# Second layer of a hybrid transformer: the compressed keys and values are worked out earlier, the router's weights and the compressed scores later

## Chip, cores and metric

The kernel runs on one core of a Trainium2 chip. The metric is the device time of one execution in microseconds (us). The kernel before took 1400.51 us as the median of three runs (1397.81 to 1400.72).

## What is computed

Two transformer layers over 256 tokens of width 1024, all in fp32. The first layer has two kinds of attention and a dense feed-forward part. The second layer, which the change touches, has block attention (heads `cq`, `ck`, `cv`), sparse attention in three branches (queries `dq`; compressed, selected and windowed keys), and a mixture of eight experts, two per token. Cut to the second layer:

```python
cq, ck, cv, dq, dkc, dvc, dks, dvs, dkw, dvw, dg = split_cols(x @ w_in, ODD_SIZES)
o_c = moba_attention(rope(cq), rope(ck), cv)
k_cmp = compress_blocks(dkc[:, tok_idx], pe[0], phi_w1[0], phi_w2[0])   # 15 blocks of 32 tokens
v_cmp = compress_blocks(dvc[:, tok_idx], pe[1], phi_w1[1], phi_w2[1])   # gelu(rows @ w1) @ w2
p_c   = masked_softmax(q @ k_cmp * scale)                               # compressed scores
o_d   = g0 * (p_c @ v_cmp) + g1 * selected(dq, dks, dvs) + g2 * window(dq, dkw, dvw)
x     = layer_norm(ALPHA * x + concat(o_c, o_d) @ w_out)
x     = layer_norm(ALPHA * x + moe(x))     # router logits, top 2 of 8 experts, swiglu of width 3584
```

With 256 tokens the selected and the windowed branch each see all causal keys.

## The kernel before

Every large matrix product is made from split operands: each weight tile of 128x1024 fp32 is loaded into a raw buffer (`raw`, `load_raw`, L123), cast to fp32r on ScalarE (`wh`, L150), and the rest is subtracted on VectorE (`wl`, L152). TensorE then makes three products per weight chunk (`mm3`, L160: L164, L165, L166) into one PSUM bank per 128 tokens. There are two groups of 128 tokens, t = 0 and t = 1. `project` (L293) does this for one slice of the input weights `od_w_in` and hands each bank to a `consume` function (`c_kv`, `c_dq`, `c_w`, `c_rope`), which applies the rotary embedding on VectorE and GpSimd, turns the result with TensorE transposes (`hps`) and copies it out.

In the second layer the calls stand at L907 to L929: the projection of keys and values (`c_kv`, 4 raw tiles), of the sparse queries (`c_dq`, 4), `router_weights` (L847: the layer norm's gain and shift rows are turned on TensorE, `rtps`, and multiplied with the router's matrix, `rsps`, both only needed for the router much later), the projection of the window's keys and values with the gates (`c_w`, 3 raw tiles: 420, 420 and 280 KB), `compress` (L704), `compressed` (L782: scores `cps` against the compressed keys, softmax into `ec`), the projection of `ck`, the start of the sparse attention (`nsa_start`, L808: scores `sps`, exp on ScalarE, turned probabilities `ptps`, product `oT`), the projections of `cq` and `cv`, the output weights, and so on to the router and the experts.

`compress` has three steps. The rows are formed: 32 small products with a selection matrix (`kp`, L710), a ScalarE copy (`km`, L714), eight VectorE copies into the gathered rows (`xr`, L721), two GpSimd operations for the border columns. Then 64 records of products with the hidden weights `phi_w1` (`hp`, L731), whose 8 raw tiles of 512 KB are loaded here (L729). Then a copy (`cmp_hs`, L734), a fold (`ht`, L737), the gelu on VectorE and ScalarE, and the products `kc` and `vc` (L757, L764), which the end of the sparse attention (`nsa_end`, L815) needs.

Three resources set the order. Raw tiles come from two pools of 4 and 6 buffers and go round (first four indices of every ten to the pool of 4): a load waits until a buffer of its pool is free, that is until the tile that was in it has been subtracted (or, for `phi_w1`, multiplied). All raw loads are issued on SyncE's one queue, in order; a load that waits holds up those behind it. The order of instructions on each engine is not the program text's: a planner puts them in order ahead of time from its own estimate of when each is ready, with earlier program text preferred. On the chip each engine then runs its list in that order. PSUM tiles outside the projections share two buffers of tag `at` (`kp`, `hp`, `ht`, `kc`, `vc`, `rsps`, `rtps`, `cps`, `ptps`) and two of tag `sp` (`hps`, `sps`).

After the second layer's attention the experts run: 672 raw tiles of 512 KB, which stream in as long as raw buffers come free.

Of the kernel before, what the change touches and what calls it, by code (L numbers as in the profile page):

```python
# [39 lines left out]
def hybrid_kernel(ctx, tc, x, ev_w_in, ev_w_out, dif_lambda, dif_subln, ffd_w_gate, ffd_w_up, ffd_w_down,  # L40
# [82 lines left out]
    def load_raw(src, kt, n):  # L123

        raws = []
        step = max(1, min(kt, 1024 // n))
        for k0 in range(0, kt, step):
            kk = min(step, kt - k0)
            raw = raw_tile()
            rv = raw[:, :kk * n]  # L130
            ld = nc.sync.dma_start(rv.rearrange("p (k n) -> p k n", n=n),
                                   src[k0 * P:(k0 + kk) * P, :].rearrange("(k p) n -> p k n", p=P))
            loads.append(ld.ins)
            raws.append((rv, kk, n))
        return raws
# [4 lines left out]
    def split_w(raws, after=()):  # L140


        ps_ = []
        for i, (rv, kk, n) in enumerate(raws):
            w = kk * n
            pool = split_pools[nsplit[0] % len(split_pools)]
            nsplit[0] += 1
            wh = pool.tile([P, 1024], F32R, tag="wh", name="wh")
            wl = pool.tile([P, 1024], F32R, tag="wl", name="wl")
            nc.scalar.copy(wh[:, :w], rv)  # L150
            with behind(after[i] if i < len(after) else None):
                nc.vector.tensor_tensor(wl[:, :w], rv, wh[:, :w].bitcast(F32), ALU.subtract)  # L152
            for k in range(0, w, n):
                ps_.append((wh[:, k:k + n], wl[:, k:k + n]))
        return ps_
# [101 lines left out]
    def bank(shape=(P, 512), name="bk"):  # L257
        return at.tile(list(shape), F32, tag="sp" if name in TAGS else "at", name=name)

    def mbank(name, tag="mm"):  # L260
        return mm.tile([P, 512], F32, tag=tag, name=name)
# [31 lines left out]
    def project(xp, src, n, consume, raws=None, after=()):  # L293
        w = split_w(raws or load_raw(src, KD, n), after)
        for t in range(NT):
            ps = mbank("mmps")
            mm3(ps[:, :n], list(zip(xp[t], w)))
            consume(t, ps)
# [52 lines left out]
    def pairs_of(r):  # L351
        return [r[:, i * P:(i + 1) * P] for i in range(r.shape[-1] // P)]
# [67 lines left out]
    xp = [x_parts(xt[:, t]) for t in range(NT)]  # L420
# [32 lines left out]
    def c_rope(to, dst, scaled, gqa=False):  # L453
        def f(t, ps):
            r = roped()
            rope(ap, ps, 8, t, r, scaled, gqa)
            to(dst, pairs_of(r), t)
        return f
# [120 lines left out]
    with more_split("splitf", "right", NSPLIT), mkpool("ffn") as fp, more_raw("rawf", NEXTRA):  # L579
# [25 lines left out]
        for k0, t in steps:  # L605
# [6 lines left out]
            if k0 + 2 == KF:  # L612
# [5 lines left out]
                if t == 0:  # L618
                    xp = [x_parts(x2[:, 0])]
# [13 lines left out]
    w1 = od_w_in[0]  # L633
# [9 lines left out]
    ckB = blocks_tile(lp, 4, "ckB")  # L643
# [57 lines left out]
            nc.vector.tensor_tensor(fold[r], ident[r, q * 32:q * 32 + 30],  # L701
                                    ident[r, q * 32 + 30:q * 32 + 31].to_broadcast([32, 30]), ALU.add)

    def compress():  # L704
        kp = bank((P, 2, 2, P), "kp")
        for z in range(2):
            for g in range(2):
                for t in range(NT):
                    for a in range(2):
                        nc.tensor.matmul(kp[a * 64:a * 64 + 64, z, g, t * 64:t * 64 + 64],  # L710
                                         kvc[:, t, z * P + g * 64:z * P + g * 64 + 64], selm[:, a],
                                         start=True, stop=True)
        km = ap.tile([P, 2, 2, P], F32, tag="rope_u", name="km", bufs=2)
        nc.scalar.copy(km, kp)  # L714
        xr = lp.tile([P, 2, 16, 32], F32, tag="e", name="xr", bufs=NE_)
        nc.gpsimd.memset(xr[:, :, :, 31], 0.0)
        nc.gpsimd.tensor_copy(xr[:, :, :, 30], peT.rearrange("p (z k) -> p z k", z=2))
        for z in range(2):
            for g in range(2):
                for jj in range(2):  # L720
                    nc.vector.tensor_copy(  # L721
                        xr[:, z, 8 * jj:8 * jj + 8, g * NCMP:(g + 1) * NCMP],
                        km[:, z, g].rearrange("p (n j) -> p j n", j=8)[:, :, jj:jj + NCMP])
        hp = bank((P, 2, S), "hp")
        for z in range(2):
            for q in range(4):
                raw = raw_tile()
                rv = raw.rearrange("p (k n) -> p k n", n=S)
                nc.sync.dma_start(rv, nsa_phi_w1[0, z, q * 512:(q + 1) * 512, :].rearrange("(k p) n -> p k n", p=P))  # L729
                for k in range(4):  # L730
                    nc.tensor.matmul(hp[k * 32:k * 32 + 32, z], xr[:, z, q * 4 + k], rv[:, k],  # L731
                                     start=q == 0, stop=q == 3, skip_group_check=True)
        hs = ap.tile([P, 2, S], F32, tag="rope_u", name="cmp_hs", bufs=2)
        nc.vector.tensor_copy(hs, hp)  # L734
        ht = bank((P, 4, 32), "ht")
        for m in range(4):
            nc.tensor.matmul(ht[:, m, :30], hs[:, m // 2, m % 2 * P:(m % 2 + 1) * P], fold, start=True, stop=True)  # L737
        hb_ = ap.tile([P, 4, 30], F32, tag="cmp_h", name="cmp_h", bufs=1)
        nc.vector.tensor_copy(hb_, ht[:, :, :30])
        u = ap.tile([P, 4, 30], F32, tag="cmp_u", name="cmp_u", bufs=1)  # L740
        nc.vector.tensor_tensor(u, hb_, hb_, ALU.mult)
        nc.vector.tensor_scalar(u, u, 0.044715, 1.0, op0=ALU.mult, op1=ALU.add)
        nc.vector.tensor_tensor(u, u, hb_, ALU.mult)
        nc.vector.tensor_scalar(u, u, -40.0, None, op0=ALU.max)
        nc.scalar.activation(u, u, AF.Exp, scale=-2.0 * math.sqrt(2.0 / math.pi))
        nc.vector.tensor_scalar(u, u, 1.0, None, op0=ALU.add)
        nc.vector.reciprocal(u, u)
        nc.vector.tensor_tensor(u, u, hb_, ALU.mult)
        gr = lp.tile([P, 2, 2, 4, 32], F32, tag="e", name="gr", bufs=NE_)
        nc.gpsimd.memset(gr, 0.0)  # L750
        nc.gpsimd.tensor_copy(gr[:, :, :, :, :NCMP],
                              u[:, 2:4].rearrange("p m (g n) -> p m g n", g=2)[:, :, :, None, :]
                              .to_broadcast([P, 2, 2, 4, NCMP]))
        kc = bank((P, 32), "kc")
        for g in range(2):
            for m in range(2):
                nc.tensor.matmul(kc[g * 64:g * 64 + 64, :NCMP], w2[:, 0, m], u[:, m, g * NCMP:(g + 1) * NCMP],  # L757
                                 start=m == 0, stop=m == 1)
        for g in range(2):
            nc.vector.tensor_copy(kcB[g * 64:g * 64 + 64, g, :NCMP], kc[g * 64:g * 64 + 64, :NCMP])  # L760
        vc = bank((P, 2, 64), "vc")
        for g in range(2):
            for m in range(2):
                nc.tensor.matmul(vc[:, g], gr[:, m, g].rearrange("p r n -> p (r n)"), w2[:, 1, m],  # L764
                                 start=m == 0, stop=m == 1)
        for g in range(2):
            nc.vector.tensor_tensor(vblk[:, g], vc[:, g, None, :].to_broadcast([P, 4, 64]),
                                    bmask[:, :, None].to_broadcast([P, 4, 64]), ALU.mult)
# [78 lines left out]
    def router_weights():  # L847

        ps = bank((P, 2, NE), "rsps")
        for i, row in enumerate(gb):  # L850
            for k0 in range(0, KD, 4):
                pt = bank((P, 4, P), "rtps")
                for k in range(4):
                    nc.tensor.transpose(pt[:, k], row[:, (k0 + k) * P:(k0 + k + 1) * P], ident)
                rT = lp.tile([P, 4, P], F32, tag="pT", name="rowT", bufs=3)
                evac(rT, pt)
                for k in range(4):
                    nc.tensor.matmul(ps[:, i], rT[:, k], wr[:, k0 + k], start=k0 + k == 0, stop=k0 + k == KD - 1)
                if i == 0:
                    nc.vector.tensor_tensor(gwr[:, k0:k0 + 4], wr[:, k0:k0 + 4], rT[:, :, :NE], ALU.mult)  # L860
        nc.vector.tensor_copy(s1, ps[:, 0])
        nc.vector.tensor_tensor(s0, ps[:, 1], br, ALU.add)
# [42 lines left out]

    rbank = bank
    project(xp, w1[:, 2048:2560], 512, c_kv, None, (normed[-2],) * 3 + (normed[-1],))  # L907
    project(xp, w1[:, 1536:2048], 512, c_dq)
    router_weights()
    project(xp, w1[:, 2560:2840], 280, c_w)  # L910
    compress()
    ec = compressed()
    project(xp, w1[:, 512:1024], 512, c_rope(to_blocks, ckB, False))
    os_ = [nsa_start(qt) for qt in range(NT)]
    project(xp, w1[:, 0:512], 512, c_rope(to_heads, cqT, True))
    project(xp, w1[:, 1024:1536], 512, lambda t, ps: nc.scalar.copy(cv[:, t], ps))
# [391 lines left out]
```

## Time and profile before

| what | value |
|---|---|
| median of three runs | 1400.51 us |
| profiled execution, device time | 1402.62 us |
| its span on the core | 1400.8 us |
| TensorE busy | 1314.0 us (94%) |
| VectorE busy | 754.3 us (54%) |
| ScalarE busy | 544.7 us (39%) |
| bytes moved | 429.98 MB |
| second layer, first projection to first expert's products | about 332 to 519 us of the span |

The profile's times are us from the span's start. Matmuls overlap, so that a row's duration is longer than its distance to the next start; idle time of an engine ahead of an instruction stands in square brackets behind it, with what ended it.

### The profile page before, as it was taken

The page shows a single profiled execution, that of the slowest core. Times are in us where ns is not written, and L with a number is a line of the kernel's source. Part 1 is how long each engine was busy: PE and PEld are TensorE (multiplying, and loading weights), DVE is VectorE, ACT ScalarE, POOL GpSimd, SP SyncE. Part 2 cuts the span into 40 slices and gives each one's busy share as a digit, 9 for nine tenths or more (in the row PEclk, how much of TensorE's full clock was granted, in tenths as well). Part 3 has the DMA queues.
Part 4 walks back from the last instruction along what each step waited for, and adds up shares of the span by engine and source line. Part 5 has one row for each costly group of instructions (what it writes and reads, how often), then busy time and mean ns, then how long its engine had stood idle before and what let it go on. Part 6 is the DMA issues. An engine that isn't in the chain of part 4 may idle for free. (4 is left out here: it accounts for less than half of the span.)

```text
span 1400.8 us, 18207 instructions
## 1 busy us (share of the span) xinstructions
PE 1314.0 (94%) x6136; PEld 848.2 (61%) x6136; DVE 754.3 (54%) x1194; ACT 544.7 (39%) x796; POOL 45.2 (3%) x79
## 2 busy tenths in 40 slices
PE   8979999998988989999999999999998999999983
PEld 7856888886864763367874356884446886432221
DVE  5977655547578561278863057893137895201004
ACT  4454444433436311166652056772034774100000
POOL 2200000001210000000000000000000000000000
PEclk9999999999999989999999999999999999999996
DMA  9244646545543399899999999999999998999992
GB/s 348 74 135 137 225 149 211 181 121 178 161 150 121 124 362 399 333 408 409 402 355 399 402 409 409 401 408 384 405 406 409 407 389 329 409 402 409 409 402 108
DMA packets 146805, 429.98 MB, mean 307 GB/s; under 512 B 15696, under 2 KB 23280, under 8 KB 146704
## 3 DMA queue, kind: packets, MB, share of 16 engines
q1 hardware_dynamic: 146000, 426.48, 80.3%
q0 software_dynamic: 704, 2.26, 0.5%
q8 instruction: 50, 0.82, 0.2%
q14 instruction: 51, 0.42, 0.1%
HBM read 427.64 MB, written 1.05 MB: 306 GB/s over the span
## 5 line engine op out<-in xcount | busy, mean ns | idle before, releaser
L152 DVE TENSOR_TENSOR wl<-raw,wh 128x1024 fp32r<-128x1024 f32 x378 | 456.0, 1225 | 116.0 <-ACT wh L150 113.0
L150 ACT CAST wh<-raw 128x1024 fp32r<-128x1024 f32 x378 | 390.1, 1046 | 230.1 <-PE pg L166 67.7
L1124 PE MATMUL pgu<-raw,xs 128*64 128x512 f32 x1120 | 267.4, 608 | 5.1 <-DMA raw<-in_moe_w_up_dram 4.3
L1124 PEld LDWEIGHTS pgu<-raw,xs 128*64 128x64 f32 x1120 | 81.7, 139 | 166.6 <-issue 130.1
L1169 PE MATMUL y<-raw,hT_s 128*64 128x512 f32 x560 | 132.9, 605 | 6.8 <-DMA raw<-in_moe_w_down_dram 5.9
L1132 DVE TENSOR_TENSOR h_s<-h_s,pgu 64x512 f32<-64x512 f32 x35 | 24.1, 690 | 185.3 <-ACT h_s L1131 185.1
L1169 PEld LDWEIGHTS y<-raw,hT_s 128*64 128x64 f32 x560 | 37.9, 138 | 95.3 <-issue 61.7
L1131 ACT ACTIVATE h_s<-pgu 64x512 f32<-64x512 f32 x35 | 20.7, 590 | 175.7 <-PE pgu L1124 175.7
L164 PE MATMUL mmps<-wh,xTh 128*128 128x512 f32 (+2 forms) x192 | 77.4, 404 | 1.0 <-ACT wh L150 0.8
L166 PE MATMUL mmps<-wh,xTl 128*128 128x512 f32 (+2 forms) x192 | 76.2, 399 | 1.8 <-DVE xTl L173 1.7
L165 PE MATMUL mmps<-wl,xTh 128*128 128x512 f32 (+2 forms) x192 | 75.0, 393 | 0.5 <-DVE wl L152 0.5
L164 PE MATMUL pg<-wh,xeh 128*128 128x512 f32 x168 | 71.0, 422 | 1.9 <-ACT wh L150 1.6
L165 PE MATMUL pg<-wl,xeh 128*128 128x512 f32 x168 | 69.3, 413 | 2.3 <-DVE wl L152 2.3
L166 PE MATMUL pg<-wh,xel 128*128 128x512 f32 x168 | 68.8, 409 | 0.0
L164 PE MATMUL y<-wh,hTh 128*128 128x512 f32 x168 | 66.6, 396 | 0.8 <-ACT wh L150 0.8
L165 PE MATMUL y<-wl,hTh 128*128 128x512 f32 x168 | 66.5, 396 | 0.9 <-DVE wl L152 0.8
L166 PE MATMUL pu<-wh,xel 128*128 128x512 f32 x168 | 66.8, 398 | 0.0
L165 PE MATMUL pu<-wl,xeh 128*128 128x512 f32 x168 | 66.7, 397 | 0.0
L166 PE MATMUL y<-wh,hTl 128*128 128x512 f32 x168 | 66.3, 394 | 0.0
L164 PE MATMUL pu<-wh,xeh 128*128 128x512 f32 x168 | 65.4, 389 | 0.0
L327 DVE COPY hT_s<-tps 128x256 f32<-128x256 f32 x17 | 7.2, 424 | 101.5 <-PE tps L1151 101.5
L325 ACT COPY hT_s<-tps 128x256 f32<-128x256 f32 x18 | 6.7, 372 | 135.1 <-PE tps L1151 135.1
(376 smaller groups left out, 1912.8 us busy)
## 6 DMA issues: line engine op xcount, KB each, us to landing
raw<-in_moe_w_up_dram SPq DMA_DIRECT2D x224, 512.0 KB, 10.1
raw<-in_moe_w_gate_dram SPq DMA_DIRECT2D x224, 512.0 KB, 10.1
raw<-in_moe_w_down_dram SPq DMA_DIRECT2D x224, 512.0 KB, 10.1
raw<-in_ffd_w_gate_dram SPq DMA_DIRECT2D x22, 512.0 KB, 5.1
raw<-in_ffd_w_up_dram SPq DMA_DIRECT2D x22, 512.0 KB, 4.4
raw<-in_ffd_w_down_dram SPq DMA_DIRECT2D x22, 512.0 KB, 4.7
raw<-in_ev_w_in_dram SPq DMA_DIRECT2D x20, 512.0 KB, 8.9
raw<-in_od_w_in_dram SPq DMA_DIRECT2D x20, 512.0 KB, 4.2
```

The source lines that it names most:

```text
L150: nc.scalar.copy(wh[:, :w], rv)
L152: nc.vector.tensor_tensor(wl[:, :w], rv, wh[:, :w].bitcast(F32), ALU.subtract)
L164: nc.tensor.matmul(ps, ah, wh, start=first and i == 0, stop=False)
L165: nc.tensor.matmul(ps, ah, wl, start=False, stop=False)
L166: nc.tensor.matmul(ps, al, wh, start=False, stop=last and i == n - 1)
L325: nc.scalar.copy(dst, src)
L327: nc.vector.tensor_copy(dst, src)
L1124: nc.tensor.matmul(p_[i * SMALL:(i + 1) * SMALL], xs[:, k0 + k], halves(w[k], n)[j], start=k0 + k == 0, stop=k0 + k == KD - 1)
L1131: nc.scalar.activation(h[:SMALL], p_[:SMALL], AF.Silu)
L1132: nc.vector.tensor_tensor(h[:SMALL], h[:SMALL], p_[SMALL:], ALU.mult)
L1169: nc.tensor.matmul(ys[0][i * SMALL:(i + 1) * SMALL], ts[k], w[:, i * 512:(i + 1) * 512], start=c0 == 0 and k == 0, stop=c0 + n == F_EXP an ...
```

## The change

`compress` is cut in two: `compress_rows` forms the rows, `compress` takes them and does the rest. Five calls of the second layer stand in another order. No instruction is added or taken away.

```diff
-    def compress():
+    def compress_rows():
+
         kp = bank((P, 2, 2, P), "kp")
...
                         km[:, z, g].rearrange("p (n j) -> p j n", j=8)[:, :, jj:jj + NCMP])
+        return xr
+
+    def compress(xr):
         hp = bank((P, 2, S), "hp")
...
     project(xp, w1[:, 2048:2560], 512, c_kv, None, (normed[-2],) * 3 + (normed[-1],))
+    xr = compress_rows()
     project(xp, w1[:, 1536:2048], 512, c_dq)
+    compress(xr)
+    project(xp, w1[:, 2560:2840], 280, c_w)
     router_weights()
-    project(xp, w1[:, 2560:2840], 280, c_w)
-    compress()
+    project(xp, w1[:, 512:1024], 512, c_rope(to_blocks, ckB, False))
     ec = compressed()
-    project(xp, w1[:, 512:1024], 512, c_rope(to_blocks, ckB, False))
     os_ = [nsa_start(qt) for qt in range(NT)]
```

## Rows read from the trace of the kernel before

**Rows 1.** The page: busy times, and the share of the load queue

```profile
PE 1314.0 (94%) x6136; PEld 848.2 (61%) x6136; DVE 754.3 (54%) x1194; ACT 544.7 (39%) x796; POOL 45.2 (3%) x79
q1 hardware_dynamic: 146000, 426.48, 80.3%
```

**Rows 2.** Busy times by stage (stretch: length, engines, granted clock, DMA share, GB/s)

```profile
350.00:363.00 13.00, 13.00 (x68) 10.83 (x67) 7.88 (x16) 4.12 (x10) 4.50 (x7) 1.00 0.70 222
...
386.90:397.50 10.60, 5.44 (x73) 3.67 (x73) 6.27 (x16) 1.37 (x2) 1.33 (x2) 0.89 0.84 243
395.10:401.90 6.80, 6.06 (x18) 5.18 (x19) 4.73 (x11) 1.65 (x3) 2.84 (x4) 0.50 1.05 339
412.00:438.00 26.00, 26.00 (x123) 17.88 (x122) 20.29 (x51) 15.96 (x52) 1.41 (x2) 1.00 0.31 92
438.00:449.00 11.00, 7.17 (x30) 3.38 (x29) 10.30 (x20) 7.49 (x25) 0.00 (x0) 1.00 0.67 214
```

**Rows 3.** SyncE's waits by what ended them, 430 to 620 us

```profile
SPq L131 <- PE pgu L1124: 30.7, 16, 9.5
SPq L131 <- PE oT L823: 26.5, 1, 26.5
SPq L131 <- DVE pT L327: 11.7, 1, 11.7
```

**Rows 4.** TensorE in order of time, 362 to 416 us (start, us, engine, line, operation)

```profile
363.01 0.63 PE L333 MATMUL hps<-ident,roped 128*128 128x128 f32 x4
...
380.64 1.15 PE L710 MATMUL kp<-selm,kvc 128*64 128x64 f32 x32
...
389.24 3.66 PE L731 MATMUL hp<-raw,xr 128*32 128x256 f32 x64 [2.22 <-DVE xr L721]
395.84 1.89 PE L737 MATMUL ht<-fold,cmp_hs 128*128 128x30 f32 x8 [2.94 <-DVE cmp_hs L734]
...
415.55 1.86 PE L787 MATMUL cps<-kcB,dqT 128*128 128x30 f32 x16
```

**Rows 5.** ScalarE and VectorE around the compression, 384 to 396 us

```profile
384.62 2.00 ACT L150 CAST wh<-raw 128x1024 fp32r<-128x1024 f32 x2 [3.44 <-DMA raw<-in_od_w_in_dram]
386.64 0.59 ACT L714 COPY km<-kp 128x512 f32<-128x512 f32 x1
...
388.57 1.51 DVE L721 COPY xr<-km 128x120 f32<-128x120 f32 x8
...
393.87 1.23 DVE L152 TENSOR_TENSOR wl<-raw,wh 128x1024 fp32r<-128x1024 f32 x1 [3.19 <-ACT wh L150]
395.01 0.68 DVE L734 COPY cmp_hs<-hp 128x512 f32<-128x512 f32 x1
```

**Rows 6.** SyncE's loads: merged, then three single ones (narrow windows)

```profile
336.51 17.38 SPq L729 DMA_DIRECT2D raw<-in_nsa_phi_w_dram  x8
...
369.02 0.37 SPq L131 DMA_DIRECT2D raw<-in_od_w_in_dram  x1
...
374.91 0.37 SPq L131 DMA_DIRECT2D raw<-in_od_w_in_dram  x1
...
380.72 0.37 SPq L131 DMA_DIRECT2D raw<-in_od_w_in_dram  x1
```

**Rows 7.** DMA issues in 330:360, then 360:392 (count, KB each, median us to landing)

```profile
raw<-in_nsa_phi_w_dram SPq DMA_DIRECT2D x8, 512.0 KB, 7.3
...
raw<-in_od_w_in_dram SPq DMA_DIRECT2D x9, 512.0 KB, 3.5
```

**Rows 8.** TensorE's larger group of the router's weights, 344 to 390 us (busy, mean ns)

```profile
L858 PE MATMUL rsps<-wr,rowT 128*128 128x8 f32 x32 | 3.9, 240 | 0.0
```

**Rows 9.** ScalarE and VectorE behind the first projection, 350 to 358 us

```profile
350.32 0.37 ACT L662 COPY kvc<-mmps 128x256 f32<-128x256 f32 x1 [0.31 <-PE mmps L166]
...
357.05 0.69 DVE L308 TENSOR_TENSOR rope_a<-mmps,rt 128x512 f32<-128x512 f32 x1 [3.33 <-ACT roped L654]
```

**Rows 10.** TensorE: the first score product of the softmax stage

```profile
412.22 1.03 PE L367 MATMUL sps<-ksB,drT 128*128 128x256 f32 x4
```

## Prediction, made before the changed kernel was built

> **What bounds the kernel now.** I read the page first [rows 1]. TensorE is busy for 94% of the span and the load queue for 80.3%, so neither alone is the bound everywhere; the stage decides. The busy times by stage come next [rows 2]: in the second layer's projections TensorE is busy without a break (13.00 of 13.00 us from 350 to 363, 26.00 of 26.00 from 412 to 438), with two exceptions: 386.9 to 397.5, where it does 5.44 us of work in 10.60, and 438 to 449, where it does 7.17 in 11.00. So here TensorE sets the pace except in these two places.
>
> Does time saved here reach the end? The experts behind it load 672 tiles, and SyncE's waits tell what that stream waits for as it starts [rows 3]: 26.5 us for the last products of the second layer's sparse attention (L823), 11.7 us for a copy of the block attention's probabilities (L327), 30.7 us in 16 waits for the first expert's own products (L1124). All of these come after the stages above and move with them. So I take it that a microsecond saved before 449 us is a microsecond saved at the end.
>
> What happens from 386.9 us on is seen on TensorE in order of time [rows 4]. It waits 2.22 us ahead of the 64 hidden products for `xr`, works on them for 3.66 us, and waits 2.94 us ahead of the fold for `cmp_hs`. The other engines show why [rows 5]. The small products of the rows were done at 381.8 us (380.64 plus 1.15, rows 4), but the copy `km` starts at 386.64: ScalarE's list has two casts before it, and these waited 3.44 us for a load. `xr` follows at 388.57. After the hidden products the copy `cmp_hs` starts at 395.01, behind a subtraction that waited 3.19 us for another cast, again of a late tile. The loads are late because of buffers [rows 6]: the tiles of `phi_w1` were issued from 336.51 us on and stay until the hidden products read them after 389 us, so three of the four buffers in the first pool are locked for some 45 us, and the projection's tiles come through the fourth one after another, at 369.02, 374.91 and 380.72, about 6 us apart.
>
> The idle time has a second price: from 395.1 to 401.9 us the granted clock is 0.50, the 1.2 GHz level, against 1.00 in the stages around it [rows 2]. TensorE works only 5.44 of the 10.60 us from 386.9 to 397.5, in which the clock falls.
>
> **The change part by part.** No product is added, so TensorE's work is the same, and only idle time and clock can change.
>
> Removed, first step: the wait of 2.22 us. Second step: the wait of 2.94 us [rows 4]. Third step: the half clock. In that stretch TensorE works 6.06 of 6.80 us [rows 2]; at the full clock the same work takes half, so 3.03 us are lost. That the factor is two can be seen from like products: the fold's 8 records take 1.89 us at half clock, 16 records of `cps` with the same 30 columns 1.86 us at the full one [rows 4]. Sum: 2.22 + 2.94 + 3.03 = **8.19 us**. What the third step brings back is not certain: the clock fell after the two waits with the 3.66 us of narrow products between them, and if these count as too little work by themselves, the half clock stays. Bounds: 0 to 3.03 us returned; I take all of it, because in the new place dense projection products stand right before and behind.
>
> Moved, the rows: `kp`, `km`, `xr`. The kv values are copied out at 350.32 plus 0.37 us [rows 9]; `kp` 1.15, `km` 0.59 and `xr` 1.51 us [rows 4, 5] give 354 us at the earliest, and VectorE idles 3.33 us up to 357.05 [rows 9], which covers `xr`. GpSimd, with its border columns, is busy 4.50 of 13.00 us there [rows 2]. They are needed when the second projection ends, about 363 us, where its last transposes stand [rows 4]; so there are some 9 us to spare. A repetition of the 4.9 us by which `km` was late (381.8 to 386.64) would still be hidden: 0, and 0 to 4.9 us if that cover were gone.
>
> Moved, the 8 loads of `phi_w1`, past three loads of `c_w` on SyncE's queue. They land a median 7.3 us after issue in this crowded stretch [rows 7]; the last was issued at about 353.5 us [rows 6] and would now be issued no later, so its data is there by about 361, in time for products at 363. Two of the `c_w` tiles then land where the last `phi_w1` tiles landed before, near 359 to 361 us. The third needs a buffer that a `phi_w1` tile has, so it waits for the first eighth of the hidden products, 363 + 3.66/8 = 363.5 us; with the 3.5 us that loads take once the queue is empty [rows 7], a cast of 1.04 (by the pair of casts in 2.00) and a subtraction of 1.23 us [rows 5] it is ready at 369.2. Queued behind it on SyncE are all tiles of `ck`, `cq`, `cv` and the output weights. Until then TensorE has the rest of the hidden products, to 366.7 us, and three quarters of `c_w`'s products (two of three tiles, six of eight chunks), and `router_weights`, whose larger group alone is 3.9 us busy [rows 8]. Cost 0; if the cover is missing, 369.2 - 366.7 = 2.5 us. The gain on the other side is that all eight buffers come free by 367 us, so that the tiles behind are no longer passed through one buffer; nothing more is counted for that, since TensorE has no further idle time there.
>
> Moved, the fold, gelu, `kc`, `vc`: the gelu's chain is only needed at the end of the sparse attention, about 465 us. Moved, `router_weights`: TensorE filler in both places, needed by the router near 490. Moved, `compressed`: as before it stands ahead of the softmax stage. All three 0, if the softmax stage doesn't take them in (below).
>
> The second gap, 438 to 449: 11.00 - 7.17 = 3.83 us idle [rows 2], the scores waiting for exps. The softmax stage begins at 412.22 us [rows 10]. If it begins earlier by more than the projections do, projection products are left to fill this gap; bounds 0 to 3.83 us of further gain. I take 0.
>
> Sum: the profiled execution took 1402.62 us, 1.8 more than its span of 1400.8; less 8.19 that is 1394.4. It lies 2.1 us above the median of the three runs, 1400.51, so for the median **1392.3 us**. With the bounds: 1392.3 - 3.8 = 1388.5, and 1392.3 + 3.03 + 2.5 = 1397.8.
>
> **The rivals.** (a) *Slower: the softmax stage becomes the bound.* VectorE is busy 10.30 of 11.00 us from 438 to 449 and 20.29 of 26.00 before [rows 2]. If the planner lets `ck`'s copies, the router's copies and the compressed scores pile up just ahead of that stage, it starts at 412 us or later as now, TensorE's 8.19 us are waited away in it, and the vector work that is pushed into it adds its time: the nearest row is the compression's own stretch from 386.9 to 397.5, with 6.27 us of VectorE work, of which the 0.70 us that VectorE has free from 438 to 449 takes up little. 1400.5 + 6.27 - 0.70 = 1406.1. It decides when the first scores do not start before 412. For it: VectorE is nearly full there. Against: `ck`'s weights come sooner, and so its rotated keys and the scores. (b) *Absorbed.* The same without the pile: scores start earlier by half, 4 us are lost; 1396 to 1400.5. (c) *The planner keeps its order:* the text's order is only a preference, and `kp`, whose data was there at 351, came only at 380.64 [rows 4], behind the router's products, which use the two buffers of its tag. If it does so again, nothing changes: 1400.5. Against: in the new text `kp` comes before everything that could hold both buffers. (d) *The stream decides.* If the experts' loads alone set the end, nothing in front of them counts: 1400.5; rows 3 speak against it, since the stream waits for the second layer's products. The Trainium skill ("Perfetto Trace Analysis", section Identifying the Most-Contended Engine) advises to judge TensorE by its weight loads rather than by matmul busy time, and to optimize the most contended engine first. By that rule, with weight loads at 61% and the load queue at 80.3% [rows 1], it would be this rival; the waits of rows 3 don't agree.
>
> **How the numbers follow.** Forecast 0.66, with 1388.5 to 1397.8 as its own range; (a) 0.16; (b) 0.10; (c) 0.05; (d) 0.03. About 0.2%, 2.8 us, is what a measurement of this kernel can tell from no change. Faster by more than that: the forecast and a third of (b), 0.69. Within: the rest of (b), (c) and (d), 0.15. Slower: (a), 0.16. The range for 8 in 10 leaves out (a) and a little below the forecast's low end, where the second gap and the slack of the loads add up: 1388.0 to 1403.0.
>
> **What would show it.** Right: `kp` near 351 us, hidden products near 363 with no idle ahead of them, none ahead of the fold, a granted clock of 1.00 through to 438, first scores some 8 us or more before 412, first expert's products earlier by the same. Wrong: idle ahead of `c_w`'s last chunk (the third tile), hidden products still after 380, scores at 412, or a half-clock stretch behind the hidden products in their new place. The forecast fails as a whole if the experts' products start 8 us earlier and the end doesn't move.

## The result, and the profile after

The changed kernel takes 1393.88 us as the median of six executions (1391.54 to 1395.18), against 1400.62 us for six of the kernel before, run beside them (1397.81 to 1404.07). The ratio is 0.9947, with a 95% interval from 0.9932 to 0.9962: 5.3 to 9.5 us less. The forecast was 1392.3 us in a range from 1388.0 to 1403.0. The profiled execution took 1395.12 us, with a span of 1393.3.

The first reading is one of milestones, the start of an instruction in the two profiled executions:

| us from the span's start | before | after | difference |
|---|---|---|---|
| first product of the first projection | 332.72 | 331.90 | -0.82 |
| first hidden product `hp` | 389.24 | 363.07 | -26.17 |
| first score `sps` of the softmax stage (its mask product, just ahead of [rows 10]) | 412.01 | 399.06 | -12.95 |
| last projection product | 436.41 | 425.47 | -10.94 |
| first product of the output weights | 472.60 | 469.09 | -3.50 |
| first expert product `pgu` | 518.83 | 515.37 | -3.46 |
| end of the span | 1400.84 | 1393.34 | -7.50 |

Eleven microseconds are ahead at the last projection product, three and a half at the first expert product, seven and a half at the end; 0.8 us of each were there at the first projection product, ahead of the change. So something takes 7 us back, and something else gives 4 us; both need an explanation. What has hardly changed are the page's totals:

```profile
PE 1311.1 (94%) x6136; PEld 844.4 (61%) x6136; DVE 754.3 (54%) x1194; ACT 545.1 (39%) x796; POOL 47.3 (3%) x79
q1 hardware_dynamic: 146000, 426.48, 80.5%
```

They answer [rows 1]: 2.9 us less of TensorE's products, 3.8 us less of its weight loads, 2.1 us more of GpSimd, the rest as before. Totals over the span don't show a change of 7 us; stages do. The same view as in [rows 2] of the changed kernel (stretch: length, busy time of PE, PEld, DVE, ACT, POOL, granted clock, DMA share, GB/s), with one stretch of its own, 421.28 to 424.69:

```profile
350.00:363.00 13.00, 13.00 (x82) 10.23 (x80) 6.88 (x21) 4.10 (x8) 2.48 (x3) 1.00 0.57 176
...
386.90:397.50 10.60, 10.60 (x56) 8.88 (x55) 8.61 (x16) 3.28 (x4) 3.15 (x4) 1.00 0.01 2
412.00:438.00 26.00, 23.45 (x99) 14.75 (x99) 17.93 (x40) 14.42 (x35) 0.00 (x0) 0.88 0.46 137
421.28:424.69 3.41, 3.41 (x10) 2.63 (x9) 3.12 (x13) 3.31 (x9) 0.00 (x0) 0.50 0.37 132
438.00:449.00 11.00, 9.14 (x36) 3.64 (x34) 7.04 (x20) 5.97 (x22) 0.00 (x0) 0.98 0.05 20
```

The hole from 386.9 to 397.5 is closed: 10.60 us of work in 10.60, where there were 5.44, at a clock of 1.00. The stretch from 412 to 438, which had been full, now has 2.55 us of idle time and a half clock in two places. TensorE in order of time shows both (start, us, line, operation, idle time ahead in brackets):

```profile
349.39 0.34 PE L711 MATMUL kp<-selm,kvc 128*64 128x64 f32 x4
...
354.33 0.56 PE L711 MATMUL kp<-selm,kvc 128*64 128x64 f32 x10
...
355.08 0.80 PE L711 MATMUL kp<-selm,kvc 128*64 128x64 f32 x18
...
363.07 1.05 PE L735 MATMUL hp<-raw,xr 128*32 128x256 f32 x10
364.23 0.66 PE L333 MATMUL hps<-ident,roped 128*128 128x128 f32 x4
364.81 1.50 PE L735 MATMUL hp<-raw,xr 128*32 128x256 f32 x24
366.25 0.66 PE L333 MATMUL hps<-ident,roped 128*128 128x128 f32 x4
366.83 1.93 PE L735 MATMUL hp<-raw,xr 128*32 128x256 f32 x30
...
372.07 0.97 PE L741 MATMUL ht<-fold,cmp_hs 128*128 128x30 f32 x8
...
417.74 0.95 PE L862 MATMUL rsps<-wr,rowT 128*128 128x8 f32 x8
418.54 1.95 PE L791 MATMUL cps<-kcB,dqT 128*128 128x30 f32 x16
...
435.40 0.37 PE L364 MATMUL sps<-causalb,identb 128*128 128x256 bf16 x1 [2.55 <-ACT e L372]
```

No bracket stands at `hp` or `ht`, where [rows 4] had 2.22 and 2.94 us. But `kp` and `hp`, one group each in [rows 4], are in three pieces with other products between them, and the pieces of `hp` add up to 4.48 us instead of 3.66. The last product of a piece is what costs: from its start the next instruction took 0.49, 0.31 and 0.31 us to begin, while inside a piece products start 0.05 us apart on average. The router's products, meant to follow `c_w`, ended up beside `cps` in the softmax stage; and behind them the clock halves with no idle time ahead.

The 2.55 us at 435.40 have their cause on ScalarE, whose exps (`e`) stand in the list behind two casts of the output weights, which wait for loads:

```profile
430.38 1.04 ACT L150 CAST wh<-raw 128x1024 fp32r<-128x1024 f32 x1 [1.56 <-DMA raw<-in_od_w_out_dram]
433.38 1.04 ACT L150 CAST wh<-raw 128x1024 fp32r<-128x1024 f32 x1 [1.96 <-DMA raw<-in_od_w_out_dram]
434.34 0.47 ACT L372 ACTIVATE e<-sps,nm 128x256 f32<-128x256 f32 x1
```

This is the pattern of [rows 5], a cast of a late tile in front of a small step that others wait for, in a new place. SyncE's waits (us in total, times, longest), from 420 to 615 us, are those of [rows 3]:

```profile
SPq L131 <- PE pgu L1129: 31.7, 15, 9.6
SPq L131 <- PE oT L827: 30.2, 1, 30.2
SPq L131 <- DVE pT L327: 11.4, 1, 11.4
```

The stream of the experts still starts behind the sparse attention's last products and the first expert's own.

### The profile page after: what moved, and what is told of

It reads as the page before. It is cut to its first block, busy times and chain, and to the rows that moved or that the text cites. A ratio compares the mean times of both kernels' runs of the same rounds, so it can differ in the third digit from the quotient of the medians.

```text
span 1393.3 us, 18209 instructions
## 1 busy us (share of the span) xinstructions
PE 1311.1 (94%) x6136; PEld 844.4 (61%) x6136; DVE 754.3 (54%) x1194; ACT 545.1 (39%) x796; POOL 47.3 (3%) x79
```

## The experiments

Theory: the stall came from raw buffers that the `phi_w1` tiles hold; the new order frees them, and that is worth the 5 us of idle time and perhaps the half clock. Rivals: the rows' early place alone does it; the router's or the scores' place does it or spoils it; what the end gains behind the first expert product is another thing.

**Both kernels again, then a third time.** No edit: the two kernels on other chips.

> The kernel before, unchanged, once more beside itself. It shows how far the expert stage's length differs between two executions of one program. In the two profiles so far that stage (first expert product to the end) took 881.9 us before and 877.9 us after, so that 4.0 of the 7.5 us between the two spans fell there. Theory A (4 us there is chance, the change only acts up to the first expert product): ratio 1.000 within 0.002, first expert product again at 518.8 within 1 us, expert stage somewhere between 876 and 884 us. Theory B (the changed kernel's expert stage is shorter in itself): expert stage 881.9 within 1 us.

> The changed kernel, unchanged, once more. Theory A: first expert product again near 515.4 (3.5 us ahead of the kernel before), expert stage anywhere from 876 to 884 us, ratio near 0.9955 (some 6 us less). Theory B: expert stage 877.9 within 1 us, ratio 0.994 to 0.995.

> The kernel before, a further profiled execution. Open: how much of the 6 us between the kernels comes from the stretch behind the first expert product. There the kernel before took 881.9 and 877.8 us in its two profiled executions, the changed one 877.9 and 877.6. If the other order of the expert stage's casts and subtractions costs something each time, 879.5 us or more; if the 881.9 was an execution with slower loads, 877 to 879 us. Half clock near 395 us: there in two of three executions of these instructions so far, so that either is expected.

> The changed kernel, a further profiled execution, to stand beside the third one of the kernel before. First expert product 514 to 515.5 us, from there to the end 877 to 879 us. Theory of a lasting gain behind the first expert product: the end stands 4 us or more ahead of that of the third execution of the kernel before. Rival (only the second layer gains): 2 to 4 us.

On one chip, e1 took 1398.45 us (10 executions), e2 1393.53 (9), and 28 executions of the kernel before 1399.37; the ratio of e2 is 0.9963 (0.9947 to 0.9978). So the gain is there again, 3.1 to 7.4 us. Two of the expectations were too narrow: e1's first expert product came at 516.31 us and not at 518.8 within 1 us, e12's at 512.68 and not from 514 to 515.5, with 882.0 us behind it and not 877 to 879. In e1's trace the stall is as before:

```profile
388.93 3.66 PE L731 MATMUL hp<-raw,xr 128*32 128x256 f32 x64 [2.30 <-DVE xr L721]
395.43 1.05 PE L737 MATMUL ht<-fold,cmp_hs 128*128 128x30 f32 x8 [2.84 <-DVE cmp_hs L734]
```

but the clock behind it isn't. The stretch of e1 that answers to 395.1 to 401.9 in [rows 2]:

```profile
394.70:401.50 6.80, 6.08 (x33) 5.22 (x34) 4.03 (x10) 0.86 (x1) 2.90 (x4) 1.00 1.06 328
```

1.00, not 0.50, behind the same idle times. And e11, the same instructions once more, has 0.50 in two places, 389.6 to 393.0 (inside `hp`) and 396.4 to 399.8. The changed kernel has it near 421 and 435 in its first execution, nowhere between 103 and 499 us in e2 and e12. So where the half clock falls, and whether it falls in this layer at all, differs between executions of either kernel.

The stretch behind the first expert product differs in the same way. From there to the end the kernel before took 882.0, 877.8 and 879.1 us, the changed one 878.0, 877.6 and 882.0. The stretch in the profiled executions of before, of after and of e12, one fence each:

```profile
518.83:1400.78 881.95, 830.93 (x3721) 468.44 (x3720) 410.91 (x470) 324.42 (x381) 3.16 (x2) 0.97 0.98 382
...
1002.70:1009.50 6.80, 6.80 (x18) 2.56 (x20) 0.81 (x5) 0.11 (x1) 0.00 (x0) 0.50 1.03 409
```

```profile
515.37:1393.28 877.91, 827.05 (x3721) 465.74 (x3720) 411.43 (x470) 324.69 (x381) 3.17 (x2) 0.97 0.98 384
```

```profile
512.68:1394.65 881.97, 832.40 (x3721) 469.85 (x3720) 411.43 (x470) 324.57 (x381) 3.17 (x2) 0.96 0.97 383
```

The second column is TensorE's busy time: 830.93 and 832.40 us in the long ones, 827.05 in the short one, for the same 3721 instructions. The line for 1002.7 to 1009.5 is one of the places where before lost them, at a granted clock of 0.50. Added up over the record of the granted clock, without the last such stretch, which begins behind the experts' last product, half clock lasted 37.5 us in before and in e12 (882.0 us both), 34.1 in e11 (879.1), and 23.9 in e1, after, e2, e3 and e4 (877.6 to 878.8). So the 4 us that the first pair showed behind the first expert product were not the change: e12, the changed kernel, is as long there as before was. The half clock goes with it, and TensorE's busy time by 3.88 and 5.35 us, but not in step (e11 has 10.2 us more of it than e1 and is 1.3 us longer), so that it is the likely cause and not a shown one. The theory of a lasting gain there expected 4 us or more between e11 and e12 and got 1.4 at the end (1396.16 against 1394.71), though the first expert product was 4.4 us earlier.

**The rows alone.** Only `compress_rows` moves; the rest keeps the old order.

```diff
     xr = compress_rows()
     project(xp, w1[:, 1536:2048], 512, c_dq)
-    compress(xr)
-    project(xp, w1[:, 2560:2840], 280, c_w)
     router_weights()
+    project(xp, w1[:, 2560:2840], 280, c_w)
+    compress(xr)
```

(`compressed()` stands ahead of `ck` again, too.)

> One part alone: the rows are formed behind the first projection; the hidden products, the router's weights and the compressed scores stay where they were before. Theory A (the stall came from the copy of the rows standing behind casts that waited for late tiles): with the rows there early, the hidden products follow the window's projection, some time from 372 to 380, no idle ahead of them; the buffers come free 10 us earlier than before, and most of the 8.2 us is gained in the projections: first expert product 2 to 4 us earlier than before, about 1396. Rival (the rows were not the point; the hidden weights hold the buffers as long as the products stand behind the window's projection): the stall shrinks by less than half, 1399 to 1401.

Measured: 1398.84 us, ratio 1.0004 (0.9992 to 1.0016). No gain, and the first expert product at 517.72, among the 516.31 to 518.83 of the kernel before: the 2 to 4 us of theory A did not come. TensorE shows why:

```profile
384.74 3.66 PE L735 MATMUL hp<-raw,xr 128*32 128x256 f32 x64
...
397.49 0.76 PE L164 MATMUL mmps<-wh,xTh 128*128 128x512 f32 x1 [6.23 <-DVE rope_u L311]
```

`hp` waits for nothing now, but the projection behind it does, for 6.23 us. VectorE's `rope_u`, which ended the wait, stood behind a subtraction of a tile whose cast ScalarE had begun only when its load had come:

```profile
393.77 1.04 ACT L150 CAST wh<-raw 128x1024 fp32r<-128x1024 f32 x1 [6.97 <-DMA raw<-in_od_w_in_dram]
```

The tiles of `phi_w1` still lay in their buffers until 388 us. What the rows waited for was the symptom; moving them moves the wait. The price of the stall is set by when the hidden products give the buffers back.

**The buffers' lock by itself.** The kernel before, with seven of the eight expert runs left out (e5), and the same with only the first of the eight `phi_w1` tiles loaded (e7):

```diff
-                raw = raw_tile()
-                rv = raw.rearrange("p (k n) -> p k n", n=S)
-                nc.sync.dma_start(rv, nsa_phi_w1[0, z, q * 512:(q + 1) * 512, :]...)
+                if z == 0 and q == 0:
+                    raw = raw_tile()
+                    rv = raw.rearrange("p (k n) -> p k n", n=S)
+                    nc.sync.dma_start(rv, nsa_phi_w1[0, z, q * 512:(q + 1) * 512, :]...)
+                    nraw[0] += 7
```

> The kernel before with seven of its eight expert runs left out (only the first expert's 84 weight tiles are loaded and multiplied), so that the time ends some 100 us after the second layer and chance in the long expert stage drops out. It is the base for the three that follow; the ratio to the whole kernel means nothing. In the profiles of the whole kernels the first expert product came at 518.8 and 516.3 us; expected for this one about 516 to 519 us again.

> The cut kernel before (old order of the calls), in which only the first of the eight tiles of the hidden weights is loaded, into one raw buffer, and all hidden products read it: seven loads and their buffers are left out, the products stay. Theory A (the stall at 387 to 396 us came from the hidden weights holding three of the four buffers of a pool, so that the projections' tiles came through the fourth, and ScalarE and VectorE stood at late tiles): no wait of ScalarE for od_w_in over 2 us, the idle of 2.2 and 2.9 us ahead of the hidden products and the fold falls to under 1 us, the time falls by 4 us or more against the cut kernel before. Rival (the rows are late because the text's order has them late): the idle stays.

e5 took 622.08 us, with the first expert product at 518.04. In e7 the hidden values come from one tile alone and the routing changes with them, so that its whole time (772.53 us, with an overflow expert) says nothing; the first expert product does: 510.69 us, 7.35 earlier. Of these, 1.40 are there at the first projection product already (330.58 for 331.98), ahead of what the edit touches; the other 5.95 come after it, where executions of one kernel differ by up to 2.4 us. ScalarE's waits for tiles of the input weights from 330 to 470 us, in e5:

```profile
ACT wh L150 <- DMA raw<-in_od_w_in_dram: 13.9, 5, 7.2
```

In e7 there is no such wait, and TensorE has, with the old order of all products:

```profile
378.58 1.15 PE L710 MATMUL kp<-selm,kvc 128*64 128x64 f32 x32
384.87 3.66 PE L733 MATMUL hp<-raw,xr 128*32 128x256 f32 x64
389.44 1.05 PE L739 MATMUL ht<-fold,cmp_hs 128*128 128x30 f32 x8 [0.91 <-DVE cmp_hs L736]
```

No idle time ahead of `hp`, 0.91 us ahead of the fold. So the seven tiles were the cause, by the buffers they held or by their 3.5 MB. e5 tells the two apart: its last `phi_w1` tile landed at 359.87 us. From 369 to 387 SyncE issued one load at a time, each after a wait for an earlier tile to land and one for VectorE to be done, and the DMA share was 0.30 (the first line is SyncE's waits, the second the view of [rows 2]):

```profile
SPq L131 <- DMA raw<-in_od_w_in_dram: 9.3, 3, 3.2
...
369.00:387.00 18.00, 17.28 (x123) 14.80 (x122) 7.94 (x20) 7.70 (x12) 0.96 (x4) 1.00 0.30 89
```

At 89 GB/s, against 339 in the crowded stretch of [rows 2], the loads were not late for want of bandwidth. They were late for want of buffers.

**The change, the router's and the scores' place.** The changed kernel, cut as e5 (e6); whole and cut with `router_weights` in its old place ahead of the hidden products (e4, e8); cut with the compressed scores later (e9) and ahead of `ck` as before (e10).

```diff
 e4, e8:
     xr = compress_rows()
     project(xp, w1[:, 1536:2048], 512, c_dq)
+    router_weights()
     compress(xr)
     project(xp, w1[:, 2560:2840], 280, c_w)
-    router_weights()
 e9:
-    ec = compressed()
     os_ = [nsa_start(qt) for qt in range(NT)]
     project(xp, w1[:, 0:512], 512, c_rope(to_heads, cqT, True))
+    ec = compressed()
 e10:
-    project(xp, w1[:, 512:1024], 512, c_rope(to_blocks, ckB, False))
     ec = compressed()
+    project(xp, w1[:, 512:1024], 512, c_rope(to_blocks, ckB, False))
```

> The changed kernel with one part undone: the router's weights stand again behind the second projection (ahead of the hidden products), all else as changed. In the changed kernel the router's products were found at 392 to 418 us, inside the softmax stage, and with the compressed scores right ahead of a half-clock stretch at 421 us that no idle time precedes. Theory A (the router's work in the softmax stage costs there): no half clock at 421, scores earlier, first expert product 1 to 3 us ahead of the changed kernel's, 1391 to 1393. Rival (its place doesn't count, since the softmax stage waits for exps anyway): the same as the changed kernel within 1 us, 1393 to 1395.

> The changed kernel, cut in the same way (seven of eight expert runs left out). Theory A (all that the change gains, it gains in the second layer, and 2.7 us is what the profiles show there): the median is 2 to 3.5 us below that of the cut kernel before. Theory B (the layer gains the full 6 us that the whole kernels' medians show, the two profile pairs being unlucky): 5 to 7 us below. If 2.7 is right here, the rest of the 6 us comes in the expert stage, where the planner's lists for VectorE and ScalarE came out otherwise, too.

> The cut changed kernel with the router's weights back behind the second projection. In its whole form the profile had the first expert product at 510.1 us, 4 to 5 us ahead of the changed kernel's, but the median of the times was the same. Theory A (the router's products in the softmax stage cost 2 to 4 us there): 2 to 4 us below the cut changed kernel. Rival (that profile was a lucky one): within 1 us of it.

> The changed kernel with seven of the eight expert runs left out, and with the compressed scores called behind the projection of `cq`, two calls later. In the changed kernel, cut in the same way, the router's narrow products (`rsps`) and the compressed scores (`cps`) run one behind the other near 418 us, the granted clock is 0.50 for 3.41 us right behind them, and the softmax stage that follows the projections has 2.40 us of idle time; first expert product at 515.04 us, whole 620.05 us. Theory: the softmax stage takes the lead back because the compressed scores' copies and exps stand in ScalarE's and VectorE's lists ahead of the other scores; then with them later the last projection product comes no earlier, but the first scores do, and the first expert product comes 1 to 3 us earlier, at 512 to 514, whole 617 to 619; no half clock near 421. Rival: the stage is bound by the vector work that it holds, wherever the compressed scores stand; first expert product within 1 us of 515.0, whole 619 to 621. Second rival: the compressed softmax is then late for the end of the sparse attention; first expert product 516 or later.

> The changed kernel with seven of the eight expert runs left out, and with the compressed scores called ahead of the projection of `ck`, right behind the router's weights, as in the kernel before. This undoes the one move that no other run has undone. Theory (scores late is what lets the softmax stage take the lead back): the compressed scores come before 400 us, the first expert product 1 to 3 us earlier than 515.0, whole 617 to 619. Rival (their place doesn't matter): first expert product 514 to 516, whole 619 to 621.

Measured: e4 1393.41 us whole, as e2 on the same chip. (Its profiled execution has the first expert product at 510.13 us, but at the first projection product, ahead of all that was changed, it is 4.2 us ahead of the changed kernel's first execution already, at 327.75.) Cut, with the first expert product: e6 620.05 us (2.0 less than e5, as its theory A had it) and 515.04; e8 620.26 and 514.93; e10 619.84 and 515.13; e9 623.29 and 520.12.

e10's instructions come out in the same order as e6's on every engine, so that it is a further execution of the same work: where the scores are called, ahead of `ck` or behind it, makes no difference at all to the kernel. e8 has its hidden products 15 us later than e6, at 378.15, in one piece, and reaches the first expert product 0.1 us earlier. So no effect of the router's place shows, neither in the medians (e4 beside e2, e8 beside e6) nor in traces, whose stretch from the first projection to the experts differs by up to 2.4 us between executions of one program. e9 reaches the first expert product 5.1 us later; TensorE's waits there show the second rival:

```profile
464.01 0.27 PE L364 MATMUL sps<-causalb,identb 128*128 128x256 bf16 x1 [0.87 <-ACT e L372]
466.46 0.66 PE L822 MATMUL pcT<-ident,ec 128*128 128x128 f32 x4 [1.31 <-DVE ec L807]
```

The compressed scores run at 458.13 there, and the end of the sparse attention waits for their softmax. Fewer exps ahead of the others brought nothing: the idle time from the last projection product to the output weights is 8.64 us against 4.52 in e6. And the half clock came, at 428.4, although `rsps` and `cps` were 38 us apart; in e10, where they adjoin, it did not:

```profile
420.00:426.00 6.00, 6.00 (x38) 5.27 (x38) 4.79 (x18) 3.70 (x12) 0.00 (x0) 1.00 0.28 90
```

So these narrow products side by side don't decide it.

## Why the prediction was right, and where it was not

Of the prediction's own signs, `kp`, `hp`, the two waits and the first scores came as it said; the granted clock of 1.00 through to 438 did not in the first execution, nor did a first expert product some 8 us earlier: it was 3.5. TensorE's time from the first product of the first projection to the first one of the output weights can be taken apart for every execution: its length, the idle time in it, the half clock (half of its length is lost), and the rest, which is the work at full clock.

| order of the work | execution | length | idle | half clock | rest |
|---|---|---|---|---|---|
| before | before, e1, e11, e5 | 139.87, 137.75, 139.10, 139.83 | 13.19, 13.79, 10.36, 12.85 | 6.83, 0, 10.24, 6.83 | 123.3, 124.0, 123.6, 123.6 |
| after | after, e2, e12, e6, e10 | 137.19, 134.98, 134.86, 137.24, 137.00 | 8.63, 9.30, 9.16, 10.18, 9.92 | 6.83, 0, 0, 3.41, 3.41 | 125.2, 125.7, 125.7, 125.4, 125.4 |
| router back | e4, e8 | 136.11, 137.23 | 8.63, 11.63 | 6.83, 3.41 | 124.1, 123.9 |
| one `phi_w1` tile | e7 | 133.87 | 7.01 | 6.83 | 123.4 |

Means of the first two lines: length 139.14 and 136.25, 2.9 us less; idle 12.55 and 9.44, 3.1 less; half clock 5.97 and 2.73, which is 1.6 us less lost; rest 123.6 and 125.5, 1.9 us more. The first expert product stands at 517.6 us before (four executions, 516.31 to 518.83) and 514.5 after (five, 512.68 to 515.37), 3.1 us earlier.

- **First and second step, 5.16 us of waits: right as to cause and place.** The waits at `hp` and `ht` are gone in every execution of the changed kernel; `kp` came at 349.39 for the forecast's 351, `hp` at 363.07 for 363. e3 and e7 show the reason that the prediction gave: the lock of the buffers. But the whole idle time fell by 3.1 only: the two waits were 4.86 us on average (4.13 to 5.16 in the four executions), and behind the last projection product the idle time rose from 4.2 to 5.1 us on average, with a wait of 1.8 to 2.6 us near 435, behind casts of the output weights; the other waits inside the projections grew by 0.8. The prediction had kept that stage's idle time as a further gain of 0 to 3.83 us and not as a loss.
- **Third step, 3.03 us of clock: mis-sized.** It was read from one execution. Three of four executions of the old order have a half clock between 389 and 402 us, e1 with the same waits has none; the changed kernel has one, somewhere else, in three of five. On average 1.6 us. The lower bound of 0 was right to be kept, but for another reason than the one given: not that narrow products may be too little work, but that where half clock falls differs from execution to execution. The Trainium skill ("TensorE: Matmul & The Clock Gate", section HAM oscillation — how this bites in real kernels) explains a lower clock by TensorE's waits for loads. The half clock behind the waits at 389 and 395, which stood behind late loads, agrees with that; e1, at 1.00 behind the same 2.30 and 2.84 us, and the stretch at 421.28 with no idle time ahead, do not.
- **"TensorE's work is the same": the step that failed.** No instruction was added, but the work at full clock grew by 1.9 us, in all five executions. Between e1 and e2, both without half clock, by groups (start to next start, idle time left out): `hp` 3.66 to 4.45, `hps` 3.46 to 4.04, `kp` 1.08 to 1.48, `sps` 17.67 to 18.06, `ptps` 8.26 to 8.58, the router's together 0.3 more, against 0.9 less in the projections. `hp` and `kp` among them are now cut in pieces by others. In e4 and e8, where `hp` is in one piece again, the rest is 124.0, though e8 idles more and gains nothing by it. For `hp` the trace shows where most of the 0.79 lies: two more ends of a piece, of 0.49 and 0.31 us. That the cuts explain the other groups, too, was not tried by itself; the figures fit.
- **Order of work, not time.** The lead of 11 us at the last projection product was no such lead in time: from there to the output weights the kernel before had 36.19 us, 4.10 of them idle; the changed one 43.62, 4.68 idle. Of the 6.8 us more of work, 1.7 are lost to the half clock at 434.93; the rest are scores, turns and their products that simply stand behind the projections now (5.5 us between e1 and e2, which have no half clock there). Rival (b), in which the softmax stage takes back 4 us, was close in its result at the output weights, but not by its mechanism: the stage didn't wait 4 us longer. Rival (a), decided by the first scores at 412 or later, fell: they came at 399.06. Rival (c) fell with `kp` at 349.39.
- **`phi_w1` loads, third tile of `c_w`: right at 0.** [rows 6, 7] The third tile was issued at 358.40 and landed 2.8 us later, well ahead of the 363.5 that the prediction had for its issue, and before any hidden product had run: it did not need a buffer that a `phi_w1` tile had. TensorE never waits there.
- **Router, gelu, scores at 0: right**, by e4, e8 and e10.
- **"A microsecond saved before 449 us is one at the end": not shown wrong.** Behind the first expert product both kernels need the same time at the same amount of half clock (877.6 to 878.8 us at 23.9 us of it), however early it came. That speaks against rival (d).

So of the 8.19 us of the sum the second layer gave about 3. That the forecast still lay 1.6 us from the measured median is in part luck: the timed executions of the two kernels differ by 5 to 7 us. Where the other 2 to 4 us are stays open, and so does whether they are there. The profiled executions of the whole kernels, three of each, differ by 3.3 us at the first expert product and by 3.8 at the end on average. But 28 executions of the kernel before on one chip spread from 1395.24 to 1403.84 us, and two of its three profiled ones were short: e1's is the second fastest of its ten, and e11's (1397.93) is faster than all seven of that kernel on its chip (1398.16 to 1404.03). Three of each can't tell 3.8 us from 5 to 7. In e5 against e6 and e10, with most of the experts left out, the timed medians differ by 2.0 (622.08; 620.05 for the nine together, on two chips), where e5's own five spread from 617.31 to 625.02. The mean granted clock of the timed executions is the same, 0.970 and 0.971 on e2's chip, so the clock of the whole span isn't it. An effect of the experts' casts and subtractions, which come in another order on ScalarE and VectorE, would be a candidate; it wasn't tried.

## What to carry to other kernels

Ask of a stall not only which instruction is late, but which buffers were held so long that its neighbours' loads came one by one, and move the reader of those buffers: moving the late instruction alone (e3) only moved the wait. Count a lead at a milestone only where the work in front of it is the same, and give products that are moved between others a price for the cuts. Take clock terms, and any difference in a long stage behind the change, from several executions of each kernel.

## What the runs showed of the hardware

- The granted clock of the same instructions differs between executions. Behind the waits at 389 and 395 us it was 0.50 for 6.83 us, 1.00 throughout, and 0.50 in two stretches of 3.41 us, in three executions of the kernel before; in the expert stage half clock lasted 23.9 to 37.5 us, and the stage 877.6 to 882.0.
- The 64 hidden products (e1 and e2) took 3.66 us in one piece and 4.45 us in three pieces with transposes between them, at the same granted clock of 1.00. The instruction behind the last product of a piece began 0.31 to 0.49 us after that product's start; inside a piece products started 0.05 us apart.
- With eight tiles of `phi_w1` in the raw buffers, loads were issued one at a time, 5.8 to 6.0 us apart (e5, 368.29 to 385.90), at 89 GB/s; with one tile loaded (e7), ScalarE had no wait for tiles of the input weights.
